# Moving four row copies behind two more high parts, and one low part from VectorE to GpSimd

## The chip, the cores and the metric

The kernel runs on one core of a Trainium2 chip. A core has engines that run side by side and wait for one another through semaphores: PE (TensorE, matrix products; PEld is its loading of weights), DVE (VectorE), ACT (ScalarE), POOL (GpSimd) and SP (SyncE, which here only issues DMAs). The metric is the device time of one execution in microseconds. Every profile shown is of one profiled execution.

## What is computed

The reference is one step of a decoder trunk with two layers, for 256 rows of a prompt and 8 x 4 rows of samples, 288 rows together, 2048 wide, in float32. Only the first layer matters here. It begins with one projection, whose columns are taken apart:

```python
def project_attn(x, w_in):
    p = x @ w_in
    ...
    q = p[..., :o1].reshape(*lead, N_HEADS, HEAD_DIM)
    k = p[..., o1:o2].reshape(*lead, N_KV_HEADS, HEAD_DIM)
    v = p[..., o2:o3].reshape(*lead, N_KV_HEADS, HEAD_DIM)
    qi = p[..., o3:o4].reshape(*lead, N_IDX_HEADS, IDX_DIM)
    ki = p[..., o4:o5]
    wi = p[..., o5:]
    return q, k, v, qi, ki, wi
```

The first 32 of the 128 rows of each head of q and k are rotated (rope). For each sample row an index score picks 256 of the 2052 keys, and attention runs over these keys alone, which lie in a paged cache:

```python
        idx, valid = index_select(qi_s, wi_s, ki_s, pos_new, key_pos, k_sel)
        ...
        k_s = jnp.where(in_past, cache_k[phys, off], k_new[new_idx])
        v_s = jnp.where(in_past, cache_v[phys, off], v_new[new_idx])
        return attend_selected(q_s, k_s, v_s, valid)
```

The rest (output projection, ConvFFN, Conformer layer, second ConvFFN) lies behind the place of the change.

## The kernel before

**Products.** Weights are held as stationary 128x128 blocks, and the 288 rows stream past them. To get float32 accuracy from three faster products, each operand is split into a high part (rounded) and a low part (the rest). `gemm_gen` runs for each block xh·wh, xl·wh and xh·wl (L258, L259, L260), in this order.

**Slabs.** The weights come in slabs of 128x1024. A group of q is 512 columns wide and has eight slabs of two blocks of rows. A group of v is 256 wide and has four slabs of four. Each slab is 24 matmuls. v has two groups, so eight slabs, called v0 to v7 here; `g_v[0].slabs[3]` is v3, the last one of the first group.

**`pump`.** At the start of slab i the program loads slabs up to i + 4 (SP, L154) and splits slabs up to i + 2: ACT writes wh (L179), then DVE writes wl = raw - wh, or POOL where `s.pool` is set (L181). So at the start of v0 the slab v2 is split, and at the start of v1 the slab v3. There are three buffers of wh and wl: v3 takes those of v0, v6 those of v3. Before the change POOL makes the low parts of all slabs of the second and third group of q and of the first two slabs of the fourth, and of one slab much later.

**Order.** Every engine runs its instructions in the order in which the program issues them. Between matmuls `gemm` calls `tick`, which adds time to the credit of several lanes (at most 3.0 each). While its credit is over zero a lane issues its next step, and the cost that the step's `yield` names is taken from the credit. In the projection a tick is worth 0.3675; a slab of v has six ticks, the last one behind its last matmul. Lanes used here:

- `ev`: the rotation of a group that has just ended. `evac_rope` copies the first 32 rows of four heads to a tile of their own (ACT, L792), the whole heads to q (L794), and puts `turn` on the lane. `turn` has four steps: shuffle and two products on DVE (L797 to L799), cost 3.0; the sum (L802), cost 2.0; four copies of the rotated rows into q on ACT (L806), cost 2.0; `post`, for q a copy of the sample rows to qn on ACT (L1199). The parameter n is 0 for k and 2, 4, 6, 8 for the four groups of q. The last group's `turn` runs while v is multiplied.
- `bg`: `sample_index`. It finds the threshold of the 256 best keys by bisection (up to about 199 us in the profile), compacts the chosen keys to a list of rows (`LST`; on DVE from about 205 us), turns it with four matmuls (L1104) and writes it as idxS (L1106). In the same step it calls `kv_load(0)`, which issues on POOL the gathers (L731) of the rows of the first four positions, two gathers each, with a memset (`pause`, L847) behind each. Then `prompt_top(1)` follows on the same lane: rounds of max and replace on DVE (L1154, L1155) and the mask pm (L1159, L1160).
- `pl_`: `turn_v`, which transposes the finished groups of v (L1213) and copies them out (L1216, L1218).

**After v.** Attention opens with a second `kv_load(0)`, with room for eleven positions: 4 to 6 go to kvB (rows named kvt), 7 to 10 to the two tiles that held xh and xl (rows named kvx). For each position its keys are transposed on PE (L1352) and copied out (L1355 on DVE, L1357 on ACT); L1293 to L1299 are the prompt's scores, which read q. Later gathers follow as positions are finished (L1414).

**A model of DVE.** `k.v(us)` keeps an estimate of when DVE will be done. `k.lag` uses it in the bisection alone, and one test in the list of rows compares a time taken from it earlier. `pump` adds 1.1 for each low part that is not POOL's.

## Time and profile before

| what | us |
|---|---|
| median of 3 runs | 2585.47 |
| range of the runs | 2582.82 to 2585.9 |
| the profiled execution's own time | 2585.12 |
| its span, first to last instruction | 2583.3 |

The mean granted clock of PE over the span is 0.994 of full speed. The stretch around the change, by the windows view (busy us of each engine in the window; the DMA share is the mean over 16 DMA engines):

| window, us | PE | DVE | ACT | POOL | DMA share | what runs |
|---|---|---|---|---|---|---|
| 200 to 220 | 18.47 | 18.82 | 10.92 | 5.61 | 0.34 | end of q's third group, fourth begins, list of rows |
| 220 to 240 | 20.00 | 17.26 | 8.56 | 0.00 | 0.54 | fourth group of q, v0 |
| 240 to 264 | 23.56 | 15.84 | 8.75 | 19.36 | 0.80 | v1 to v7, gathers |
| 264 to 280 | 11.41 | 8.39 | 5.92 | 10.42 | 0.97 | attention begins, gathers |
| 280 to 300 | 19.39 | 8.27 | 9.60 | 8.29 | 0.76 | attention |

Matmuls overlap in PE's pipeline, so one that is listed with 0.30 us follows the one before it after 0.13 us. Attention ends near 393 us; then the output projection begins.

### The profile page before, as it was taken

The numbers are of one execution on the slowest core, as the hardware profiler recorded it, in microseconds if no ns is written. First come the engines' busy times: TensorE is split into PE (matmuls) and PEld (weight loads), VectorE is DVE, ScalarE is ACT, GpSimd is POOL, SyncE is SP. The second block draws the span as 40 slices with busy tenths as digits, with TensorE's granted clock in tenths as the row PEclk, the third lists the DMA queues.
The fourth block names the chain that finished last, engine by engine and source line by source line (L and its number), as shares of the span: only waits on it lengthen the run. The fifth ranks groups of instructions, "written<-read, shape, count | busy, mean of one in ns | idle before, by whom it ended". The sixth has DMA issues, their size and how long they took to land.

```text
span 2583.3 us, 48344 instructions
## 1 busy us (share of the span) xinstructions
PE 2531.4 (98%) x19597; PEld 2436.1 (94%) x19597; DVE 1610.9 (62%) x2496; ACT 1171.5 (45%) x1858; POOL 658.3 (25%) x917
## 2 busy tenths in 40 slices
PE   9999899999999999999999999999999999999997
PEld 8889559999999999999999887999999999999997
DVE  5678446686665455555659997778555444555554
ACT  4464344464443334444446444656444333444444
POOL 2153551442221101011236563353010000111123
PEclk9999999999999999999999999999999999999999
DMA  9735865555545454556555654554554445555653
GB/s 345 207 127 184 294 237 175 163 186 177 170 164 166 160 172 157 171 163 160 180 162 172 186 166 168 172 164 162 171 163 165 165 161 171 163 165 165 174 165 102
DMA packets 151503, 454.80 MB, mean 176 GB/s; under 512 B 26112, under 2 KB 46512, under 8 KB 150000
## 3 DMA queue, kind: packets, MB, share of 16 engines
q1 hardware_dynamic: 138736, 400.04, 48.5%
q0 software_dynamic: 12016, 51.09, 5.8%
q8 instruction: 153, 2.51, 0.4%
q10 hardware_dynamic: 528, 0.59, 0.1%
q14 instruction: 70, 0.57, 0.1%
HBM read 438.37 MB, written 13.30 MB: 175 GB/s over the span
## 4 chain that ended last, share of the span: by engine, by line
PE 88%; DVE 6%; ACT 2%; issue 1%; POOL 1%; DMA 1%; another core or an unknown queue 0%; SPq 0%; ACTq 0%; DVEq 0%; POOLq 0%
PE pt L260 25%; PE pt L259 25%; PE pt L258 25%; PE pg L258 2%; PE pg L260 2%; DVE wl L181 2%; PE pg L259 2%; PE tr L1352 1%; DVE cy L1816 1%; PE pt L1832 1%; PE m L1414 1%; ACT wh L179 1%; PE pg L937 1%; DVE cy L1776 0%; PE sc L1373 0%
## 5 line engine op out<-in xcount | busy, mean ns | idle before, releaser
L181 DVE TENSOR_TENSOR wl<-raw,wh 128x1024 fp32r<-128x1024 f32 (+1 forms) x707 | 882.3, 1250 | 750.9 <-ACT wh L179 745.4
L179 ACT ACTIVATE wh<-raw 128x1024 fp32r<-128x1024 f32 (+1 forms) x726 | 760.8, 1051 | 837.1 <-PE pt L259 695.3
L260 PE MATMUL pt<-xh,wl 128*128 128x288 f32 (+1 forms) x3520 | 1040.2, 295 | 3.9 <-DVE wl L181 3.8
L259 PE MATMUL pt<-xl,wh 128*128 128x288 f32 (+1 forms) x3520 | 1041.9, 296 | 0.1
L258 PE MATMUL pt<-xh,wh 128*128 128x288 f32 (+1 forms) x3520 | 1041.1, 296 | 0.9 <-ACT xh L1473 0.9
L260 PEld LDWEIGHTS pt<-xh,wl 128*128 128x128 f32 x3520 | 665.5, 189 | 6.2 <-DVE wl L181 5.9
L258 PEld LDWEIGHTS pt<-xh,wh 128*128 128x128 f32 x3520 | 662.8, 188 | 7.7 <-issue 5.4
L259 PEld LDWEIGHTS pt<-xl,wh 128*128 128x128 f32 x3520 | 663.3, 188 | 0.4 <-DVE xl L1474 0.3
L260 PE MATMUL pt<-hh,wl 128*128 128x288 f32 (+1 forms) x1664 | 495.2, 298 | 0.0
L259 PE MATMUL pt<-hl,wh 128*128 128x288 f32 (+1 forms) x1664 | 493.8, 297 | 0.0
L258 PE MATMUL pt<-hh,wh 128*128 128x288 f32 (+1 forms) x1664 | 492.4, 296 | 0.0
L1589 POOL COPY sto<-gpad 128x2 f32<-128x2 f32 x88 | 85.2, 968 | 970.7 <-ACT gpad L1582 970.5
L259 PEld LDWEIGHTS pt<-hl,wh 128*128 128x128 f32 x1664 | 313.9, 189 | 0.1
L258 PEld LDWEIGHTS pt<-hh,wh 128*128 128x128 f32 x1664 | 313.4, 188 | 0.1
L260 PEld LDWEIGHTS pt<-hh,wl 128*128 128x128 f32 x1664 | 312.8, 188 | 0.0
L258 PE MATMUL pg<-xh,wh 128*128 128x288 f32 (+1 forms) x528 | 165.4, 313 | 3.3 <-ACT wh L179 2.3
L260 PE MATMUL pg<-xh,wl 128*128 128x288 f32 (+1 forms) x528 | 157.8, 299 | 1.7 <-DVE wl L181 1.7
L259 PE MATMUL pg<-xl,wh 128*128 128x288 f32 (+1 forms) x528 | 157.8, 299 | 0.7 <-POOL raw L152 0.5
L1593 ACT ACTIVATE s<-y,pvec 128x304 f32<-128x304 f32 x88 | 48.4, 550 | 161.0 <-DVE y L1588 161.0
L258 PEld LDWEIGHTS pg<-xh,wh 128*128 128x128 f32 (+1 forms) x528 | 100.2, 190 | 13.2 <-issue 7.9
L259 PEld LDWEIGHTS pg<-xl,wh 128*128 128x128 f32 (+1 forms) x528 | 100.1, 190 | 3.9 <-issue 2.6
L260 PEld LDWEIGHTS pg<-xh,wl 128*128 128x128 f32 (+1 forms) x528 | 100.3, 190 | 2.9 <-DVE wl L181 2.9
(371 smaller groups left out, 2291.6 us busy)
## 6 DMA issues: line engine op xcount, KB each, us to landing
raw<-w SPq DMA_DIRECT2D x713, 512.0 KB, 3.5
xt<-spread SPq DMA_DIRECT2D x60, 136.0 KB, 4.3
kid<-kvt POOLq DMA_DIRECT2D x4, 1024.0 KB
kvt<-kid SPq DMA_DIRECT2D x8, 512.0 KB, 10.9
x<-xT POOLq DMA_DIRECT2D x1, 2304.0 KB
raw<-w SPq DMA_DIRECT2D x6, 384.0 KB, 3.0
out_y<-x SPq DMA_DIRECT2D x16, 144.0 KB, 1.7
hist<-scT POOLq DMA_DIRECT2D x4, 544.0 KB
```

The lines of the kernel that those rows point to most:

```text
L179: nc.scalar.activation(wh[:, :n], r[:, :n], AF.Copy)
L181: eng.tensor_tensor(wl[:, :n], r[:, :n], wh[:, :n].bitcast(F32), op=OP.subtract)
L258: nc.tensor.matmul(out, wh[:, c:c + w], xh, start=st, stop=False)
L259: nc.tensor.matmul(out, wh[:, c:c + w], xl, start=False, stop=False)
L260: nc.tensor.matmul(out, wl[:, c:c + w], xh, start=False, stop=sp)
L937: nc.tensor.matmul(p[:, :512], qb[:, pr], kx[pr][:, 512 * i:512 * i + 512], start=True, stop=True)
L1352: nc.tensor.transpose(p[:, h * 128:(h + 1) * 128], g[:, h * 128:(h + 1) * 128], ident)
L1414: nc.tensor.matmul(po[32 * h:32 * h + 16, :128], z[:, c, i, h], g[:, 512 + h * 128:640 + h * 128], start=False, stop=(i == TS - 1 and c == ...
L1589: nc.gpsimd.tensor_copy(sto[:, j, 0:2], gp[:, 256:258])
L1593: nc.scalar.activation(s[:, :304], y[:, :304], AF.Silu, bias=k.par(bc, j))
L1816: nc.vector.scalar_tensor_tensor(acc, src, w, pl if q_ == NACT else acc, op0=OP.mult, op1=OP.add)
L1832: nc.tensor.matmul(p[32 * i:32 * i + 32, :TP], dg[:, i, m - PEM], xt[:, i, 4 * (m - PEM):4 * (m - PEM) + TP], start=m == PEM, stop=m == 7, ...
```

## The change

The second `yield` of `turn`, ahead of the copies L806, is 7.0 for n == 8, the last group of q, and stays 2.0 for the others. And v3 is marked so that its low part is made by POOL; its high part stays on ACT, and `k.v(1.1)` is not called for it.

```diff
@@ -55,6 +55,7 @@
 ROPE = 0.5
+QLAG = 7.0
 VLAG = 0.25
@@ -586,6 +587,8 @@
     for g in g_q[1:]:
         for s_ in g.slabs[:8 if g is not g_q[3] else 2]:
             s_.pool = True
+    g_v[0].slabs[3].pool = True
+
     def halving(w, nk):
@@ -801,7 +804,7 @@
             yield 3.0
             nc.vector.tensor_tensor(pk, pk, sh, op=OP.add)
             k.v(0.5)
-            yield 2.0
+            yield QLAG if n == 8 else 2.0
             for m in range(4):
                 nc.scalar.activation(dst[m][0:32], pk[32 * m:32 * m + 32], AF.Copy)
             yield 2.0
```

## The prediction, made before the changed kernel was run

> **What bounds the kernel now.** I read the page first, then the stretch of the change engine by engine in the timeline, then the windows and the chain of waits behind it. The page:

> ```profile
> span 2583.3 us, 48344 instructions
> PE 2531.4 (98%) x19597; PEld 2436.1 (94%) x19597; DVE 1610.9 (62%) x2496; ACT 1171.5 (45%) x1858; POOL 658.3 (25%) x917
> PE 88%; DVE 6%; ACT 2%; issue 1%; POOL 1%; DMA 1%; another core or an unknown queue 0%; SPq 0%; ACTq 0%; DVEq 0%; POOLq 0%
> ```

> PE is busy 98% of the span and is 88% of the chain that ended last. An edit on ACT, DVE or POOL can gain only where PE waits for them, and costs wherever it makes PE wait. So the first question is whether PE waits in the eight slabs of v. I call them v0 to v7 (v3 is the slab that the diff names). These are the rows of PE around v0/v1 and at v3:

> ```profile
> 239.24 0.30 PE L260 MATMUL pg<-xh,wl 128*128 128x288 f32 x1
> 239.37 0.53 PE L1104 MATMUL pg<-con,slot 128*128 128x32 f32 x4
> 239.73 0.38 PE L258 MATMUL pg<-xh,wh 128*128 128x288 f32 x1
> ...
> 246.24 0.30 PE L258 MATMUL pg<-xh,wh 128*128 128x288 f32 x1
> 246.37 0.29 PE L259 MATMUL pg<-xl,wh 128*128 128x288 f32 x1
> 246.50 0.29 PE L260 MATMUL pg<-xh,wl 128*128 128x288 f32 x1
> ...
> 249.43 0.30 PE L258 MATMUL pg<-xh,wh 128*128 128x288 f32 x1
> ```

> In the timeline the columns are start, duration, engine, line and operation; idle time before a row stands in brackets with its releaser. No row has such a bracket. A slab is 24 matmuls: v3 runs from 246.24 to 249.43, 3.19 us. In the v stage PE never waits for the copies or for a low part, so neither edit has a PE wait to remove here. v3's low part is first needed by its third matmul, at 246.50.

> **Edit 1, the copies of rows (L806).** These are ACT's rows:

> ```profile
> 239.44 1.06 ACT L179 ACTIVATE wh<-raw 128x1024 fp32r<-128x1024 f32 x1 [0.38 <-PE pg L259]
> 242.16 1.84 ACT L806 ACTIVATE x<-rsh 32x288 f32<-32x288 f32 x4 [1.67 <-DVE rsh L802]
> 244.04 0.45 ACT L1199 ACTIVATE qn<-x 128x128 f32<-128x128 f32 x1
> 244.40 1.04 ACT L179 ACTIVATE wh<-raw 128x1024 fp32r<-128x1024 f32 x1
> 246.30 1.06 ACT L179 ACTIVATE wh<-raw 128x1024 fp32r<-128x1024 f32 x1 [0.86 <-PE pg L259]
> 249.63 0.41 ACT L1228 ACTIVATE qi<-pg 128x288 f32<-128x288 f32 x1 [1.19 <-PE pg L260]
> ```

> PE reads the rows that they write from here on:

> ```profile
> 265.80 0.44 PE L1294 MATMUL tr<-kT,x 128*128 128x128 f32 x2
> ```

> The first high part is v3's, the last two are v4's and v5's. The ev lane gains 0.3675 a tick, to at most 3.0, and v has six ticks a slab. The first step of the rotation costs 3.0 at tick 1, the second costs 2.0 at tick 2, which leaves -1.63, and the copies come five ticks later, at tick 7, the first of v1. With 7.0 the rest is -6.63: 19 ticks, tick 21, the third of v3. The copies go behind the high parts of v4 and v5, as the title says. The copy to qn (L1199) goes to tick 26, behind v6's. Four copies of 1.84 us and one of 0.45 us move and none is added. They issue no DMA. They would end near 249.2, and attention reads them from 265.80, so the new place has some 16 us of cover. ACT no longer sits 1.67 us before them, and v4's high part may start about 0.9 us earlier, for which PE is not waiting. At 247.4 to 249.2 the copies stand ahead of the copies out of v's first group (L1228), due at 249.63. Cost: 0, with ends -0.1 and +0.3 us.

> **Edit 2, the low part of v3.** It leaves DVE and goes to POOL. What decides is what POOL has ahead of it. DVE first:

> ```profile
> 239.08 1.23 DVE L181 TENSOR_TENSOR wl<-raw,wh 128x1024 fp32r<-128x1024 f32 x1 [2.21 <-ACT wh L179]
> 241.99 0.22 DVE L1106 TENSOR_SCALAR idxS<-pg 128x64 int32<-128x64 f32 x1
> 243.31 1.21 DVE L181 TENSOR_TENSOR wl<-raw,wh 128x1024 fp32r<-128x1024 f32 x1
> ...
> 248.27 1.22 DVE L181 TENSOR_TENSOR wl<-raw,wh 128x1024 fp32r<-128x1024 f32 x1
> ...
> 263.30 0.46 DVE L1226 COPY qi<-pg 128x288 f32<-128x288 f32 x1 [7.08 <-PE pg L260]
> ```

> Each engine runs in the order in which the program issues. The row at 239.08 is v2's low part, the one at 243.31 is v3's, and between them DVE writes idxS (L1106). So the list of rows is finished in the program before v3 is split. PE says the same: the four matmuls of L1104, which feed idxS, follow the last matmul of v0 (239.24) and precede the first of v1 (239.73). That is the last tick of v0, one step before `pump` splits v3. The generator step that writes idxS also calls `kv_load(0)`, which issues the gathers of four positions, two each, with a pause behind each. These eight gathers and eight pauses are therefore on POOL's queue ahead of v3's subtraction:

> ```profile
> 204.92 2.46 POOL L181 TENSOR_TENSOR wl<-raw,wh 128x1024 fp32r<-128x1024 f32 x1 [0.81 <-ACT wh L179]
> 242.49 1.05 POOL L731 DMA_INDIRECT kvt<-kvc,idxS  x1 [35.10 <-DVE pacc L1149]
> ...
> 248.80 1.50 POOL L731 DMA_INDIRECT kvt<-kvc,idxS  x1 [0.16 <-issue]
> ...
> 253.77 0.94 POOL L731 DMA_INDIRECT kvt<-kvc,idxS  x1 [0.17 <-issue]
> 254.71 0.34 POOL L847 MEMSET pause<- 128x256 int8 x1
> ...
> 264.36 0.94 POOL L731 DMA_INDIRECT kvx<-kvc,idxS  x1 [0.17 <-issue]
> ...
> 274.44 0.94 POOL L731 DMA_INDIRECT kvx<-kvc,idxS  x1 [0.17 <-issue]
> ```

> and the group of all low parts on POOL (shortest, median and longest in ns):

> ```profile
> L181 POOL TENSOR_TENSOR wl<-raw,wh x19: 2347/2397/2463, 145.4 to 1605.9; 128x1024 fp32r<-128x1024 f32 x19
> ```

> POOL is idle for 35.10 us, but that idle time ends with the gathers, and the subtraction comes after them. The first gather starts at 242.49 and the eighth at 253.77; its pause ends at 255.05. That is one end. The other end: the eight gathers from 264.36 to 274.44 stand 1.44 us apart, and 242.49 + 8 x 1.44 = 254.01. Among the first eight the one at 248.80 took 1.50 us, beside a low part on DVE from 248.27; DVE now has one low part fewer there, so I take 254.5. With 0.1 us of issue and 2.40 us for one subtraction on POOL (the median above), v3's low part is ready at 257.0, and PE's L260 starts about 257.05 instead of 246.50. **PE waits 10.55 us** (ends 254.01 + 0.05 + 2.35 = 256.4, or 9.9; 255.05 + 0.17 + 2.46 = 257.7, or 11.2).

> [...]

> DVE gets 1.21 us back. It is worth nothing to the end: DVE waits 7.08 us for PE at 263.30.

> While PE waits, v6's high part cannot start: of three buffers it takes v3's. DVE, in order, then holds v6's low part and the rounds of `prompt_top(1)` behind it. With v3 ending at 249.43 + 12.0 = 261.4 (the 12.0 is worked out below), 0.5 us of copies, 1.06 for the high part and 1.21 for the low part, v6's low part is there at 264.2. PE comes to v6 no sooner than two slabs after 261.4, at 267.8. Nothing further is late. `k.v(1.1)` falls away for v3, but the bisection that reads it is over.

> **The clock after the wait.** The nearest rows:

> ```profile
> 216.40:219.40 3.00, 1.47 (x9) 1.00 0.00 0
> 219.40:223.00 3.60, 3.60 (x17) 0.53 0.43 146
> 223.00:226.20 3.20, 3.20 (x25) 1.00 0.51 169
> ...
> 1608.80:1612.20 3.40, 1.82 (x7) 1.82 (x8) 3.37 (x9) 2.44 (x5) 1.86 (x3) 0.50 0.87 253
> 1612.20:1615.60 3.40, 3.40 (x16) 3.40 (x16) 2.15 (x4) 3.33 (x6) 1.29 (x2) 0.50 1.00 429
> ```

> The first three are windows of PE alone: length, busy time with the instructions in brackets, granted clock, DMA share, GB/s. The last two give the busy time of PE, PEld, DVE, ACT and POOL before the clock. After 1.5 us of gaps the clock is 0.53 for 3.6 us: 17 matmuls where 3.6 x 25 / 3.2 = 28 would run, so 11 x 0.133 = 1.45 us lost. After a longer wait, at 1608.8 to 1615.6, it was 0.50 for 6.8 us, at most 3.4 us lost. I take **1.45 us**, the nearer row by work, ends 0 and 3.4. The end of v moves by 12.0 us.

> **What attention gives back.** Its first rows:

> ```profile
> 276.44 0.60 ACT L1357 ACTIVATE KT<-tr 128x512 f32<-128x512 f32 x1 [4.89 <-remote]
> 276.51 0.69 DVE L1296 TENSOR_REDUCE mx<-tr 128x4 f32<-128x512 f32 x1 [3.52 <-remote]
> ...
> 290.04 0.94 POOL L731 DMA_INDIRECT kvt<-kvc,idxS  x1 [14.30 <-PE m L1414]
> ```

> and two pieces of the chain of waits there (start, length, what):

> ```profile
> 272.99 3.50 another core or an unknown queue
> ...
> 297.43 5.41 DMA kvt<-kvc,idxS
> ```

> The gathers of positions 4 to 6 come about 1.5 us later, against a PE that comes 12 us later. Those of 7 to 10 write over xh and xl, which v7's matmuls read; they can only start at 263.3 + 12.0 = 275.3 and end near 286.8, 11 us later. ACT and DVE stop together and go on at 276.4, about when the gathers end (274.44 + 0.94). If that stop ends with the gathers, it ends 1.0 us sooner against PE. I take **-1.0**, ends 0 and -3.5 (the whole 3.50 us). From 290.04 on POOL waits for PE, so the later gathers move with it.

> **Sum**, against the profiled execution (2585.12 us, 0.35 below the median of the runs, 2585.47): 0 + 10.55 + 1.45 - 1.0 = +11.0, so **2596.1 us**. Ends: 9.9 + 0 - 3.5 = +6.4, or 2591.5; 0.3 + 11.2 + 3.4 = +14.9, or 2600.0.

> **Rivals.**
> 1. *The low part of v3 does go ahead of the gathers*, as the title's "during the row list" says. Then POOL makes it at 240.5 to 242.9, right behind v3's high part, the gathers start 0.6 us later and PE waits for nothing: 2585 to 2586, no change. It turns on one step of issue: whether v3 is split before idxS. The two orders quoted (DVE's and PE's) speak against it, and nothing in the diff moves idxS. Chance 0.09, with 0.02 of it on the faster side by the runs' spread.
> 2. *Attention absorbs the wait.* Seven positions' rows lie ready, the stop of 3.50 us and the gather's 5.41 us in the chain fall away: 11.0 + 1.0 - 3.5 - 5.41 = +3.1, or 2588.2, within 0.2%. Against it: that gather belongs to the series which POOL starts at 290.04 on PE's release. Chance 0.08.
> 3. *A second late part behind the first*, such as v6's low part, which has only some 3.6 us of cover, or a longer stop in attention: over 2600.5. Chance 0.06.

> My forecast has 0.77. A change under 0.2% (5.2 us) is about what a measurement of this kernel cannot tell from none: faster 0.02, same 0.15 (the rest of rival 1 and rival 2), slower 0.83. The range, 2588 to 2600.5, takes in rival 2 and the ends of the sum and leaves out 0.15.

> **What the profile would show.** Right: a PE row on L260 near 257 with about 10.5 us idle, released by POOL's wl; POOL's wl row directly behind the eighth gather, near 254.5; L806 behind the high parts of v4 and v5; a stretch of half clock behind the wait; kvx gathers from about 275. Wrong: a POOL wl row before 243, or PE without idle time in v3 (rival 1); attention ending less than 6 us later than before, although PE waited (rival 2).

## The result, and the profile after

The changed kernel takes 2598.89 us (median of six runs, 2596.2 to 2600.76), the kernel before 2582.79 us in six runs (2581.03 to 2585.9). The ratio is 1.0057, interval 1.0047 to 1.0068: 16 us slower by the medians, 15 by the ratio, with 12 to 18 us inside the interval. The forecast was 2596.1 us (11.0 us on top of 2585.12), with 0.83 on slower.

The profiled execution took 2599.42 us. The head of its page, and the chain that ended last:

```profile
span 2597.6 us, 48342 instructions
PE 2534.0 (98%) x19597; PEld 2438.3 (94%) x19597; DVE 1612.6 (62%) x2495; ACT 1171.8 (45%) x1858; POOL 660.9 (25%) x918
...
PE 88%; DVE 6%; ACT 2%; POOL 2%; issue 2%; DMA 1%; another core or an unknown queue 0%; SPq 0%; ACTq 0%; DVEq 0%; POOLq 0%
```

The span is 14.3 us longer, while no engine's busy time rose by more than 2.6 us. The work is the same, so the time is a wait. (Lines are numbered one higher behind the new constant and three higher behind the new mark.) PE's timeline of the changed kernel shows it; columns are start, duration, engine, line, operation, and in brackets the idle time before with its releaser:

```profile
256.38 0.61 PE L261 MATMUL pg<-xh,wl 128*128 128x288 f32 x1 [11.18 <-POOL wl L182]
256.79 0.44 PE L259 MATMUL pg<-xh,wh 128*128 128x288 f32 x1
257.03 0.44 PE L260 MATMUL pg<-xl,wh 128*128 128x288 f32 x1
...
261.59 0.44 PE L261 MATMUL pg<-xh,wl 128*128 128x288 f32 x1
261.83 0.44 PE L259 MATMUL pg<-xh,wh 128*128 128x288 f32 x1
```

This is v3's third matmul. It waits for POOL's low part, and behind it the matmuls follow at 0.24 us instead of 0.13. POOL's timeline says what the low part waited for:

```profile
241.02 1.05 POOL L734 DMA_INDIRECT kvt<-kvc,idxS  x1 [35.12 <-DVE pacc L1152]
...
244.04 1.80 POOL L734 DMA_INDIRECT kvt<-kvc,idxS  x1 [0.17 <-issue]
...
246.34 1.63 POOL L734 DMA_INDIRECT kvt<-kvc,idxS  x1 [0.17 <-issue]
...
252.77 0.95 POOL L734 DMA_INDIRECT kvt<-kvc,idxS  x1 [0.17 <-issue]
253.70 0.34 POOL L850 MEMSET pause<- 128x256 int8 x1
253.98 2.36 POOL L182 TENSOR_TENSOR wl<-raw,wh 128x1024 fp32r<-128x1024 f32 x1
256.49 0.96 POOL L734 DMA_INDIRECT kvt<-kvc,idxS  x1 [0.16 <-issue]
```

The first gather stands behind 35 us of idle time, and the eighth with its pause directly ahead of the low part. The low part ends at 256.34, and PE goes on at 256.38. ACT's and DVE's timelines of the same kernel:

```profile
241.63 1.06 ACT L180 ACTIVATE wh<-raw 128x1024 fp32r<-128x1024 f32 x1 [2.60 <-PE pg L260]
244.84 1.06 ACT L180 ACTIVATE wh<-raw 128x1024 fp32r<-128x1024 f32 x1 [2.15 <-PE pg L260]
245.80 1.78 ACT L809 ACTIVATE x<-rsh 32x288 f32<-32x288 f32 x4
```

```profile
240.52 0.22 DVE L1109 TENSOR_SCALAR idxS<-pg 128x64 int32<-128x64 f32 x1
...
243.81 1.22 DVE L182 TENSOR_TENSOR wl<-raw,wh 128x1024 fp32r<-128x1024 f32 x1
...
245.93 1.23 DVE L182 TENSOR_TENSOR wl<-raw,wh 128x1024 fp32r<-128x1024 f32 x1
...
263.60 1.23 DVE L182 TENSOR_TENSOR wl<-raw,wh 128x1024 fp32r<-128x1024 f32 x1 [14.60 <-ACT wh L180]
...
275.75 0.46 DVE L1229 COPY qi<-pg 128x288 f32<-128x288 f32 x1 [7.07 <-PE pg L261]
```

The four copies stand behind the high parts of v4 (241.63) and v5 (244.84), and nothing waits for them. DVE's third low part here, v6's at 263.60, waited 14.60 us, but PE needed it only after v4 and v5.

Where the 14.3 us are, from the milestones of the two profiled executions. v's part runs from idxS to the last copy out of v on DVE (263.30 and 275.75), attention from there to the first xh of the output projection (394.1 and 406.7):

| part | before, us | after, us | difference |
|---|---|---|---|
| start to idxS | 241.99 | 240.52 | -1.5 |
| idxS to v copied out | 21.31 | 35.23 | +13.9 |
| attention | 130.8 | 130.95 | +0.2 |
| the rest of the span | 2189.2 | 2190.9 | +1.7 |

The 13.9 us are the wait and the clock behind it. v3's third matmul would have started at 246.50 - 1.47 = 245.03 and started at 256.38: 11.35 us. (The bracket says 11.18 because idle time counts from the listed end of the matmul before.) The windows of PE in the changed kernel (length, busy time with instructions, granted clock, DMA share, GB/s):

```profile
248.80:256.30 7.50, 0.00 (x0) 0.50 0.88 309
256.38:261.83 5.45, 5.44 (x22) 0.50 0.72 229
262.40:265.83 3.43, 3.43 (x29) 1.00 0.02 6
```

The clock is at half when PE goes on at 256.38, and stays there until 262.41, for 6.03 us. From v3's third matmul to the first of v4 it takes 5.45 us; before, it took 249.43 - 246.50 = 2.93. That is 2.5 us more, and 11.35 + 2.5 = 13.9.

### The profile page after: what moved, and what is told of

It reads as the page before. It is cut to its first block, busy times and chain, and to the rows that moved or that the text cites. A ratio compares the mean times of both kernels' runs of the same rounds, so it can differ in the third digit from the quotient of the medians.

```text
span 2597.6 us, 48342 instructions
## 1 busy us (share of the span) xinstructions
PE 2534.0 (98%) x19597; PEld 2438.3 (94%) x19597; DVE 1612.6 (62%) x2495; ACT 1171.8 (45%) x1858; POOL 660.9 (25%) x918
## 3 DMA queue, kind: packets, MB, share of 16 engines
q8 instruction: 153, 2.51, 0.4%
## 4 chain that ended last, share of the span: by engine, by line
PE 88%; DVE 6%; ACT 2%; POOL 2%; issue 2%; DMA 1%; another core or an unknown queue 0%; SPq 0%; ACTq 0%; DVEq 0%; POOLq 0%
PE pt L261 25%; PE pt L260 25%; PE pt L259 25%; PE pg L259 2%; PE pg L261 2%; DVE wl L182 2%; PE pg L260 2%; PE tr L1355 1%; DVE cy L1819 1%; PE pt L1835 1%; PE m L1417 1%; ACT wh L180 1%; PE pg L940 1%; POOL kvt L734 0%; PE sc L1376 0%
## 5 line engine op out<-in xcount | busy, mean ns | idle before, releaser
L260 PE MATMUL pt<-xl,wh 128*128 128x288 f32 (+1 forms) x3520 | 1042.6, 296 | 0.1
L259 PE MATMUL pt<-xh,wh 128*128 128x288 f32 (+1 forms) x3520 | 1041.7, 296 | 0.9 <-ACT xh L1476 0.9
L259 PEld LDWEIGHTS pt<-xh,wh 128*128 128x128 f32 x3520 | 663.4, 188 | 7.7 <-issue 5.3
L260 PEld LDWEIGHTS pt<-xl,wh 128*128 128x128 f32 x3520 | 663.9, 189 | 0.4 <-DVE xl L1477 0.3
L260 PE MATMUL pt<-hl,wh 128*128 128x288 f32 (+1 forms) x1664 | 493.7, 297 | 0.0
L259 PE MATMUL pt<-hh,wh 128*128 128x288 f32 (+1 forms) x1664 | 492.3, 296 | 0.0
L260 PEld LDWEIGHTS pt<-hl,wh 128*128 128x128 f32 x1664 | 313.9, 189 | 0.1
L259 PEld LDWEIGHTS pt<-hh,wh 128*128 128x128 f32 x1664 | 313.4, 188 | 0.1
L261 PE MATMUL pg<-xh,wl 128*128 128x288 f32 (+1 forms) x528 | 158.4, 300 | 12.7 <-POOL wl L182 11.2
L259 PE MATMUL pg<-xh,wh 128*128 128x288 f32 (+1 forms) x528 | 166.0, 314 | 3.0 <-ACT wh L180 2.1
L260 PE MATMUL pg<-xl,wh 128*128 128x288 f32 (+1 forms) x528 | 158.4, 300 | 0.7 <-POOL raw L153 0.5
L261 PEld LDWEIGHTS pg<-xh,wl 128*128 128x128 f32 (+1 forms) x528 | 101.1, 191 | 14.4 <-POOL wl L182 11.4
L259 PEld LDWEIGHTS pg<-xh,wh 128*128 128x128 f32 (+1 forms) x528 | 100.8, 191 | 12.9 <-issue 7.9
L260 PEld LDWEIGHTS pg<-xl,wh 128*128 128x128 f32 (+1 forms) x528 | 100.9, 191 | 3.9 <-issue 2.6
```

Of the source, the lines that this page charges most:

```text
L259: nc.tensor.matmul(out, wh[:, c:c + w], xh, start=st, stop=False)
L260: nc.tensor.matmul(out, wh[:, c:c + w], xl, start=False, stop=False)
L261: nc.tensor.matmul(out, wl[:, c:c + w], xh, start=False, stop=sp)
```

## The experiments

The theory to test: the loss is made by POOL's queue alone, that is by the gathers and pauses issued ahead of v3's subtraction, with a clock term behind the wait. Rivals: the copies have a share; any low part on POOL at this time is too slow; the wait depends on DVE's work beside POOL rather than on the number of gathers. The experiments ran on three chips, and chips differ: the kernel before takes 2565 us on two of them (in the kernels profiled there attention is 18 to 19 us shorter) and 2583 on the third. So each ratio is to the kernel before on the same chip. Diffs are against the changed kernel, and in the last group (e7 to e10) against the kernel before.

**The change again** (c1; no edit to the changed kernel; chip of 2582.96 us).

> The changed kernel as it is, on the chip of the next three. Theory: PE waits about 11 us in v3 and then runs at half clock for some 6 us; 12 to 17 us slower than the kernel before.

Measured: 2595.74 us, ratio 1.0049 (1.0033 to 1.0066). PE waits 11.18 us for POOL's low part, and idxS to v copied out takes 35.1 us. The loss repeats.

**The copies alone** (e1; chip of 2565.40 us).

```diff
-    g_v[0].slabs[3].pool = True
```

> The copies of the last group moved, the low part of v3 left on DVE. Theory (the whole loss comes from v3's low part standing behind eight gathers on POOL): no wait of PE in v, time within 2 us of the kernel before. Rival A (moving the copies delays the copies out of v's first group and the transposes behind them): PE idle of 0.5 us or more before the transposes of v, and 1 us or more lost.

Measured: 2564.86 us, ratio 0.9998 (0.9989 to 1.0008). PE has no wait in v, and v's part takes 21.3 us as before. The first edit costs nothing and brings nothing.

**The low part alone** (e2; same chip).

```diff
-            yield QLAG if n == 8 else 2.0
+            yield 2.0
```

> v3's low part on POOL, the copies where they were. Theory: PE waits 10 to 11.5 us at the third matmul of v3, then runs at half clock for 3.4 to 6.8 us; 13 to 17 us slower than before, as the whole change. Rival A: no more than 13 us, the rest being the copies' share.

Measured: 2577.95 us, ratio 1.0051 (1.0034 to 1.0067). PE's timeline of this kernel:

```profile
256.09 0.61 PE L261 MATMUL pg<-xh,wl 128*128 128x288 f32 x1 [11.26 <-POOL wl L182]
```

The loss belongs to the second edit. By the medians it is 12.6 us, just under the 13 to 17 that were expected and where rival A would have it. But the whole change, repeated, lost no more (12.8 us on its chip), and the copies alone lost nothing, so nothing is left for the copies. v's part is 34.2 us, 1 us less than with both edits: the clock came back sooner (at 259.06, 2.97 us behind the restart instead of 6.03), not the low part.

**The gathers behind the low part** (e3; same chip; a step is put between idxS and its gathers, so that v3 is split first).

```diff
         nc.vector.tensor_scalar(idxS, p[:, :64], 0.25, None, op0=OP.add)
+        yield 0.4
         kv_load(0)
```

> The whole change, but the first eight gathers are issued one lane step later (a yield of 0.4 between idxS and kv_load), so that v3's low part stands ahead of them on POOL. Theory (order on POOL's queue): POOL makes it right behind v3's high part, in about 2.4 us, PE does not wait, the gathers start at most 1 us later; time within 2 us of the kernel before. Rival B (POOL is too slow for a low part beside DVE's work, 2.4 us against 1.2): PE still waits for it, 2 us or more.

Measured: 2565.15 us, ratio 0.9996 (0.9987 to 1.0006), and PE has no wait in v. POOL's and DVE's timelines of this kernel:

```profile
240.32 2.40 POOL L182 TENSOR_TENSOR wl<-raw,wh 128x1024 fp32r<-128x1024 f32 x1 [33.24 <-ACT wh L180]
244.31 1.05 POOL L734 DMA_INDIRECT kvt<-kvc,idxS  x1 [1.59 <-DVE pacc L1153]
```

```profile
240.44 2.59 DVE L801 TENSOR_TENSOR rsh<-rsh,con 128x288 f32<-128x288 f32 x1
242.96 0.45 DVE L802 TENSOR_TENSOR rsh<-rsh,con 128x288 f32<-128x288 f32 x1
...
243.81 0.21 DVE L1109 TENSOR_SCALAR idxS<-pg 128x64 int32<-128x64 f32 x1
```

The same subtraction on the same engine, issued one step ahead of the gathers instead of behind them, and the 13 us are gone: POOL makes it in its idle time. Its price is on DVE. L801 took 2.59 us where its twin L802 takes 0.45; it started with POOL's subtraction and ended 0.3 us behind it. Measured from PE's rows, idxS and the gathers came 2.1 us later for it, where at most 1 was expected; the measured time does not show it.

**The slab before** (e4; same chip; v2 instead of v3, which is split ahead of idxS).

```diff
-    g_v[0].slabs[3].pool = True
+    g_v[0].slabs[2].pool = True
```

> The whole change, but the mark is on v2 instead of v3: v2 is split before idxS in the program, so its low part falls into the time of the row list. Theory: no wait of PE in v; DVE no longer waits for v2's high part ahead of the rotation and idxS, so idxS and the gathers come up to 1 or 2 us earlier; 0 to 3 us faster than before. Rival B: PE waits 2 us or more for v2's low part, and the time is 3 us or more over the kernel before.

Measured: 2565.62 us, ratio 1.0001 (0.9991 to 1.001), no wait of PE in v. POOL's and DVE's timelines:

```profile
238.82 2.38 POOL L182 TENSOR_TENSOR wl<-raw,wh 128x1024 fp32r<-128x1024 f32 x1 [31.81 <-ACT wh L180]
241.37 1.05 POOL L734 DMA_INDIRECT kvt<-kvc,idxS  x1 [0.16 <-DVE pacc L1152]
```

```profile
239.69 1.66 DVE L1152 SCALAR_TENSOR_TENSOR pacc<-con,pacc 128x128 f32<-128x128 f32 x1
```

In e3 and here the low part on POOL stands ahead of the gathers and is in time, so the second rival falls. It also brings nothing: idxS came 2.0 us and the first gather 0.7 us earlier against PE's rows, as expected, but PE waits for neither in v. Again an instruction of DVE ends only with POOL's (L1152 took 0.28 us in the changed kernel).

**Four gathers (e5), and two (e6), instead of eight** (chip of 2582.96 us; the first `kv_load(0)` has room for two positions, then for one).

```diff
-    kvt = {"pos": 0, "done": 0, "cap": 4}
+    kvt = {"pos": 0, "done": 0, "cap": 2}
```

> The whole change with room for two positions instead of four in the first kv_load, so that four gathers stand ahead of v3's low part. Theory (queue): each gather with its pause is 1.44 to 1.6 us, so PE's wait falls from 11.2 to between 4.8 and 5.4 us; with half clock behind it the loss is 5 to 9 us. Rival C (the wait is set by something other than the number of gathers ahead, such as the transfers of the gathered rows): PE's wait stays over 8 us.

> The same with one position, two gathers ahead. Theory: v3's low part is ready about 242.5 + 2 x 1.5 + 2.4 = 247.9 on the clock of the profile before, PE waits 1.2 to 2.2 us; with or without a stretch of half clock the loss is 1 to 4 us. Rival C: over 8 us of wait.

Measured with four: 2591.48 us, ratio 1.0032 (1.0021 to 1.0044). With two: 2586.49 us, ratio 1.0013 (1.0004 to 1.0023). PE's timelines, of four gathers and of two:

```profile
250.70 0.61 PE L261 MATMUL pg<-xh,wl 128*128 128x288 f32 x1 [5.45 <-POOL wl L182]
```

```profile
244.81 0.40 PE L261 MATMUL pg<-xh,wl 128*128 128x288 f32 x1 [1.07 <-POOL wl L182]
```

The wait is 11.18, 5.45 and 1.07 us for eight, four and two gathers. From four to eight it grows by 5.73, or 1.43 for each gather with its pause: the spacing of an undisturbed gather, as the prediction had it. From two to four it grows by 4.38, because those two gathers were stretched by DVE's low parts (1.80 and 1.64 us instead of 0.94). So the number of gathers sets the wait, and DVE's work beside them adds to it. The losses, 8.5 and 3.5 us by the medians, lie in the expected bounds; the waits, 5.45 and 1.07, lie just outside theirs (4.8 to 5.4 and 1.2 to 2.2). With two gathers left the profile shows only 1.3 us of it (v's part is 22.65 us instead of 21.31); that execution, of 2582.01 us, was the fastest of its kernel, and where the rest is lost is not shown. There POOL and DVE met the other way round; their timelines in that kernel:

```profile
242.36 2.40 POOL L182 TENSOR_TENSOR wl<-raw,wh 128x1024 fp32r<-128x1024 f32 x1
```

```profile
242.35 3.50 DVE L182 TENSOR_TENSOR wl<-raw,wh 128x1024 fp32r<-128x1024 f32 x1
```

DVE's low part of v4, otherwise 1.22 us, took 3.50 us beside POOL's of v3, the 2.40 us of POOL and 1.1 more.

**A place where DVE is late.** At 217 us, where the fourth group of q begins, PE waits for splits before the change too: 0.80 us for a high part on ACT, 0.73 us for a low part on DVE, and half clock behind, from 219.57 to 222.98. Four kernels try the two ideas of the change there: the copies of the third group later, alone (e7); with a third slab of the fourth group on POOL (e8); with one round of the row list on DVE later, so that a low part goes ahead of it (e9); and with no slab of the fourth group on POOL (e10).

```diff
-            yield 2.0
+            yield 3.0 if n == 6 else 2.0
```

e8, chip of 2582.96 us, has this and

```diff
-        for s_ in g.slabs[:8 if g is not g_q[3] else 2]:
+        for s_ in g.slabs[:8 if g is not g_q[3] else 3]:
```

> The kernel before, with both kinds of edit put where its profile has PE waiting (216.8 to 218.8): the copies of the third group of q (n == 6) one high part later, and the low part of the third slab of q's fourth group on POOL, which is idle there and has no gather queued yet. Nothing of the change itself. Theory: PE's two waits of 0.80 and 0.73 us go, and the stretch of half clock behind them, 1.4 us more; 2 to 4 us faster than the kernel before. Rival D (the half clock is not caused by these waits): 1 to 2 us faster, the clock still half near 219.

Measured: 2583.58 us, ratio 1.0002 (0.9992 to 1.0012). The gain that was expected did not come. PE's, POOL's and DVE's timelines:

```profile
217.67 0.40 PE L260 MATMUL pg<-xh,wl 128*128 128x288 f32 x1 [1.95 <-DVE wl L181]
```

```profile
208.51 2.83 POOL L181 TENSOR_TENSOR wl<-raw,wh 128x1024 fp32r<-128x1024 f32 x1 [2.44 <-ACT wh L179]
```

```profile
209.11 2.51 DVE L1067 TENSOR_SCALAR m__2430<-x__2408 128x511 int32<-128x511 int32 x1
```

The two waits became one of 1.95 us for the next low part on DVE. The low part given to POOL freed 1.21 us of DVE and held an instruction of DVE (0.43 us in the kernel before) until POOL was done, some 2.1 us. The other three ran together on a chip of 2565.22 us. e7 has the first of these diffs alone:

> The kernel before with the copies of the third group of q (n == 6) one high part later, and nothing on POOL. Theory: the high part of q's slab is early, but its low part stands on DVE behind two rounds of the row list; PE's two waits near 217 (0.80 and 0.73 us) become one of about 1.1 us; 0 to 2 us faster than the kernel before.

Measured: 2563.69 us, ratio 0.9995 (0.9986 to 1.0004); ACT's wait is gone and DVE's is 1.00 us. e9 has it and

```diff
-LST = (2.2, 2.2, 2.2, 1.5, 1.2, 0.9, 5.0)
+LST = (2.2, 2.2, 2.2, 1.5, 1.2, 0.9, 3.5)
...
-            yield LST[3]
+            yield 3.0 if b == 1 else LST[3]
```

> The same, and one round of the row list moved behind that low part (3.0 instead of 1.5 after the second round, and 3.5 instead of 5.0 at the end of the list). Nothing goes to POOL. Theory: no wait of PE near 217 or one under 0.2 us, no half clock behind it; 2 to 4 us faster than the kernel before (0.08 to 0.15%, at the edge of what five rounds can tell).

Measured: 2562.23 us, ratio 0.9989 (0.998 to 0.9998). e10 has the diff of e7 and

```diff
-        for s_ in g.slabs[:8 if g is not g_q[3] else 2]:
+        for s_ in g.slabs[:8 if g is not g_q[3] else 0]:
```

> The copies of n == 6 one high part later, and the first two slabs of q's fourth group taken off POOL and given to DVE (1.2 us each). Theory E (a DVE instruction that starts while POOL makes a low part is held until POOL is done: 2.25 us for a tile of 32x4 elements in the profile before, ending with POOL's row): those rows fall to under 0.8 us, DVE is not later than before although it does two low parts more, PE's waits near 217 go or stay under 0.3 us; 1 to 4 us faster than the kernel before. Rival (those DVE rows are long by themselves): they stay over 2 us, DVE is 2.4 us later, and PE's wait near 217 grows to 3 us or more.

Measured: 2562.84 us, ratio 0.9988 (0.9979 to 0.9997). Neither e9 nor e10 has a wait of PE near 217 or half clock behind it. e10 is the opposite of the change's idea: it takes two low parts away from POOL and gives DVE 2.4 us more to do. DVE's timeline of the kernel before, then of e10:

```profile
201.88 2.78 DVE L1037 SCALAR_TENSOR_TENSOR eq<-scr,need,eq 128x516 int16<-128x516 int16 x1
204.69 0.43 DVE L1038 TENSOR_TENSOR gt<-gt,eq 128x516 int16<-128x516 int16 x1
205.16 2.25 DVE L1040 TENSOR_SCALAR new<-gt 32x4 bf16<-32x4 int16 x1
```

```profile
201.91 0.74 DVE L1037 SCALAR_TENSOR_TENSOR eq<-scr,need,eq 128x516 int16<-128x516 int16 x1
202.69 0.43 DVE L1038 TENSOR_TENSOR gt<-gt,eq 128x516 int16<-128x516 int16 x1
203.15 0.17 DVE L1040 TENSOR_SCALAR new<-gt 32x4 bf16<-32x4 int16 x1
```

Two instructions beside POOL's low parts fell from 2.78 and 2.25 us to 0.74 and 0.17. That returns 4.1 us to DVE for 2.4 us of work taken on. e9 and e10 are 3.0 and 2.4 us faster than the kernel before, with intervals that almost reach 1. That is about what the prediction's rows had there, 1.5 us of waits and 1.45 of clock, but the clock's part is not in every execution with a wait there: before and after have half clock behind their two waits (219.57 to 222.98, 218.03 to 221.45), and e7, with 1.00 us, and e8, with 1.95, have full clock from 215 to 224 us. So what the gain is made of is only in part shown. Which of the two is better can't be told.

## Why the prediction came out as it did

The direction and the mechanism were right, and the time came 2.8 us above the forecast, inside the range. That it came so near is in part luck: the forecast adds 11.0 us to an execution of 2585.12 us, and the kernel before came to 2582.79 over six runs, so the change cost 16.1 us by the medians. Between the two profiled executions it cost 14.3, which is 3.3 over the sum: 0.8 in the wait, 1.05 in the clock, 1.2 in attention and 0.2 outside the sum.

- **Copies, 0.** Right: 0.9998 alone. Even the place, behind the high parts of v4 and v5, was as counted.
- **Order of issue.** Right, and it decided the case. The first rival (low part ahead of the gathers) fell with POOL's row at 253.98; e3 and e4 show that its price, no change, would have been right had it held. (The title does not have the words that this rival quotes from it; its argument does not need them.)
- **The wait, 10.55 us.** It was 11.35, just past the upper end of 11.2. The term that was mis-sized is the gathers' time. From the first gather to the end of the eighth's pause it took 253.70 + 0.34 - 241.02 = 13.02 us; the prediction had 12.0. It took the stretched gather to be rarer with one low part fewer on DVE. In fact the low parts of v4 and v5 came earlier (243.81, 245.93) and each caught the start of a gather: 1.80 + 1.63 against 2 x 0.94 is 1.55 us over eight undisturbed spacings of 1.44 (11.5).
- **The clock, 1.45 us.** It was 2.5, inside its ends of 0 and 3.4. In the row chosen, PE had restarted at full clock and then ran 3.41 us at half; here it restarted at half clock and stayed there for 6.03 us. In e2 and e5 the term was 1.4 and 1.6 (v's part less 21.3 and less the wait), with 2.97 and 3.42 us of half clock behind the restart. So in these three kernels the term has a spread of about 1 us, and it goes with how long the clock stayed at half.
- **Attention, -1.0 us.** It came to +0.2, just outside the ends. The stop did end 1.0 us sooner against PE. By the timeline DVE went on at 276.51 before and at 287.93 after, 11.4 us later, while v was copied out 12.45 us later. But PE waited 1.64 us up to 286.36 and 2.46 us up to 289.47, and the granted clock was half from 289.7 to 293.1. PE's row of the changed kernel, then its windows behind the stop, before and after:

```profile
289.47 0.93 PE L1355 MATMUL tr<-ident,kvt 128*128 128x128 f32 x4 [2.46 <-DVE KT L1358]
```

```profile
276.50:280.00 3.50, 2.64 (x22) 1.00 0.97 298
280.00:283.50 3.50, 3.50 (x40) 1.00 1.02 408
```

```profile
287.93:291.00 3.07, 1.45 (x7) 0.79 0.97 342
291.00:294.50 3.50, 3.50 (x27) 0.70 1.04 418
```

  In the second window of each pair, both 3.50 us long, 27 instructions against 40 are 1.1 us: the gain is spent. The repeated run of the change shows half clock at the same place (288.1 to 291.5). One step of the reasoning failed: the gathers of positions 4 to 6 were to come 1.5 us later. The last four of them, issued from 258.62 on before, came from 269.44 on, behind 10.23 us in which POOL waited for nothing that the profile shows. Why is open; the stop ended with the later kvx gathers all the same.
- **Second rival (attention absorbs it).** Fell: the gather of 5.4 us is in the chain as before, 12.6 us later with the rest.
- **Third rival (a second late part).** v6's low part ended at 264.83 (forecast 264.2), in time.
- **What was not in the sum.** The start of the profiled execution before was 1.5 us slower, the rest 1.7 us faster. At the start it is half clock from 14.8 to 18.2 us, which the execution after didn't meet. In the rest, after had one more wait of PE, of 0.69 us at 1364.41 (0.9 us), one 0.2 us longer, and half clock behind that one (1.5 us); 0.9 us came back later. This pair of rows is the second wait, PE's timeline of before and of after at the same matmul:

```profile
1391.03 0.40 PE L260 MATMUL pt<-xh,wl 128*128 128x290 f32 x1 [2.09 <-DVE wl L181]
```

```profile
1404.71 0.40 PE L261 MATMUL pt<-xh,wl 128*128 128x290 f32 x1 [2.29 <-DVE wl L182]
```

  In the kernel before, the granted clock stayed at 1.00 in the 4 us behind the wait; in the changed kernel it fell to 0.50 for about 3.4 us. The length of a wait alone did not set its half clock: of two other waits at one and the same matmul, both of 4.71 us, the one that ended at 1610.38 in the kernel before has 6.83 us of half clock around its end and the one that ended at 1624.74 in the changed kernel has 3.41.

## What to carry to other kernels

Idle time of an engine is free only for an instruction that stands ahead of what ends that idle time: ahead of the gathers, in e3, the low part cost nothing (ratio 0.9996), and behind them PE waited 11.35 us for it. Count the engine's queue at the place in the program where the moved instruction is issued, each DMA issue and pause in it, before you price the instruction itself. A low part moved from VectorE to GpSimd is not simply taken off VectorE: here it made some instructions of VectorE 1.4 to 2.3 us longer; look at what will run beside it. And the three waits of PE of 5.45 to 11.35 us (e5, e2 and the change) cost 1.4 to 2.5 us of half clock on top.

## What the runs showed of the hardware

**VectorE held by GpSimd.** While POOL's subtraction ran, some DVE instructions ended only behind it: 0.17 us became 2.25 (32x4 elements), 0.43 became 2.51, 0.45 became 2.59, 0.28 became 1.66, 1.22 became 3.50. In these rows how much of POOL's 2.4 us was left decided, and the instruction's own length came on top: each of them ended behind POOL's row by its own length less 0.13 to 0.15 us (1.22 us long, 1.09 behind; 0.17 long, 0.03 behind). The other way round, the two gathers of the changed kernel that started beside a low part on DVE ended 0.81 us behind it: 244.04 + 1.80 = 245.84 against 243.81 + 1.22 = 245.03, and 247.97 against 247.16. L385 and L997 of DVE ran beside POOL's low part at their usual length. Two rows of the timeline of the kernel before show an instruction of the kind and size of L801 (TENSOR_TENSOR, 128x288), with one input, pt, that PE wrote:

```profile
1605.87 2.35 POOL L181 TENSOR_TENSOR wl<-raw,wh 128x1024 fp32r<-128x1024 f32 x1 [9.15 <-ACT wh L179]
1606.12 0.46 DVE L385 TENSOR_TENSOR lnt<-pt,lnt 128x288 f32<-128x288 f32 x1 [1.75 <-ACT lnt L384]
```

It took 0.46 us, where L801 took 2.59. The reductions of the bisection (L997) took 0.75 us beside POOL's low parts and without them. Two of the held ones have a single input tensor (L1040, 32x4, and L1067, 128x511), so the number of inputs alone does not tell the held ones from the others. What does was not shown.
